# Opening of a flow-matching backbone: TensorE's order written out by hand, one filter or operand step behind each pair of modulation blocks, result tiles from two pools

## The chip, the cores and the metric

One core of a Trainium2 chip. The metric is device time in microseconds (us), lower is better; the profile is of one execution.

## The reference

One trunk layer for 128 context tokens and 256 latent tokens of width 2048, all in float32: a SwiGLU half step, a mixer (Hyena convolutions and gated DeltaNet), a second SwiGLU half step. Each sub-layer is wrapped in norms and in a modulation that comes from a conditioning vector by one large matrix. What the opening needs of it:

```
mod = silu(c) @ ada_w + ada_b                         # 2048 x 18432, for c and for c_ctx
h   = rms_norm(x, norm_pre[0]) * (1 + mod[1]) + mod[0]
x   = x + 0.5 * mod[2] * rms_norm((silu(h @ wg) * (h @ wu)) @ wd, norm_post[0])
# the Hyena filters depend on weights alone:
f    = sin(feats @ w1 + b1); f = sin(f @ w2 + b2); f = (f @ w3) * (exp(-t * |decay|) + 0.05)
spec = rfft(taps(f) / sum|taps(f)|)                   # two orders, 1024 channels, for n = 128 and 256
```

## The kernel before

A framework records the instructions in program order, then a planner orders each engine's queue by a simulated timeline, hands out tiles of the pools and sets the semaphores. `issue_after(ins)` keeps a block's instructions behind `ins` on that engine's queue; it adds no wait for a result.

The opening does three things before the first FFN can start.

- **The modulation's first two sets** (`first_mods`, L306). Shift and scale of the first sub-layer are 64 blocks of 128x1024 (512 KB) of `ada_w`, loaded on SP's queue (`first_blocks`, L292, issue L301). They lie in nine buffers, three of each of the tags that later hold the FFN's weights (raw, hi, lo). There are two passes `g` of 16 steps `kt`; each takes two blocks and multiplies them by the two conditioning vectors (L323: four matmuls, eight records in the profile, four column groups of one result tile `ada`). After a pass the result is copied by ACT (L329), transposed (L332) and turned into factors on DVE; then six `modulate` calls (L455) transpose a 128x512 piece of the tokens (L461), apply the factors on DVE (L471), and split the result into a high part on ACT and a low part on POOL (L122, L123). A pass's half of the operands `hh`, `hl` is then ready; the FFN takes the first half first.
- **The filters** (`filters`, L685). A small two-layer network of sines (L727, `sine` L667), then four turns (two orders, two halves of the channels). A turn has three steps over time pieces `t`: four matmuls into two result tiles (L759, L760), two evictions on DVE (L762), a row set to zero on POOL (L765), sum and difference on DVE (L767, L768), absolute values on ACT (L770, L771) and their sum (L772). Then come the norms (L780, eight matmuls of one column) and the spectra (L790 with ACT copies L791; L798 with ACT copies L799 and DVE L801, L802). Six stores of 256 KB a turn go to device memory (`put`, L785) from ACT's queue. The last layer's columns `w3` are loaded on POOL's queue (L707), and each turn begins by splitting its columns (L745, L746). The tiles `fh`, `wf`, `w3` have one buffer, `fev` two.
- **Tokens and small vectors** (`load_x` L256, `setup` L177). The token rows come on SP's queue behind the first four blocks. Of the small vectors the first two come on SP, the others on POOL's queue, recorded after the first yield of `setup`.

`first_mods` calls `next(work)` once behind each `kt`: three filter steps, then the vectors, then the tokens, then the filters' remaining steps. That places the work in program order only; which of them TensorE does first is the planner's choice, apart from the four matmuls of a `kt`, which are tied in pairs. Result tiles are 128x512 banks of PSUM: `aux()` (L115) takes them from a pool of three, `acc()` and `ada` from a pool of five.

The FFN's weights follow on SP's queue (L149), the first of them behind the load of block 56 and behind the filters' network (`gate`). Each unit of 512 KB is split by ACT (L122) and DVE (L123) and used in 24 matmuls (L156 to L158).

Of the kernel before, what the change touches and what calls it, by code (L numbers as in the profile page):

```python
# [11 lines left out]
F32 = mybir.dt.float32  # L12
# [7 lines left out]
P = 128  # L20
D = 2048
KT = D // P
NP_ = 128
NS = 256
T = NP_ + NS
# [8 lines left out]
HID = 64  # L34
# [70 lines left out]
class Builder:  # L105
    def __init__(self, ctx, tc, ins, outs):
        self.ctx, self.tc, self.nc = ctx, tc, tc.nc
        self.I, self.O = ins, outs
        self.side, self.rate, self.credit, self.gate, self.gd, self.hold = None, 0.0, 0.0, [], {}, None

# [3 lines left out]

    def aux(self, name="aux"):  # L115
        return self.psa.tile([P, 512], F32, tag="aux", name=name)

# [59 lines left out]
    def setup(self):  # L177
# [35 lines left out]
        o = 0  # L213
# [10 lines left out]
        for i, dst, src in loads:  # L224
            if i < 2:
                nc.sync.dma_start(out=dst, in_=src)

        def vectors(g):
            a, b = starts[g], starts[g + 1]
            pt = self.aux()  # L230
            nc.tensor.transpose(pt[:, :b - a], rt[:b - a, g, :], self.ident[:b - a, :b - a])
            nc.vector.tensor_copy(out=vec[:, a:b], in_=pt[:, :b - a])


# [7 lines left out]
        yield  # L242
        for i, dst, src in loads:
            if i >= 2:
                nc.gpsimd.dma_start(out=dst, in_=src)
        for g in range(1, len(starts) - 1):
            vectors(g)
        nc.vector.tensor_scalar(out=self.vec["gconv"], in0=self.vec["gconv"], scalar1=0.5, scalar2=None, op0=ALU.mult)
# [4 lines left out]
        nc.vector.tensor_scalar(out=self.vec["onorm"], in0=self.vec["onorm"], scalar1=0.5, scalar2=None, op0=ALU.mult)  # L253
        yield

# [49 lines left out]

    def first_mods(self, pool, blocks, hh, hl, work):  # L306


        nc = self.nc
        ab = pool.tile([P, 2, KT], F32, name="ab0")  # L310
        pre = self.vec["pre"]
        for g in range(2):

            pa = self.psm.tile([P, 512], F32, tag="mm", name="ada")
            for kt in range(KT):
                aw = [next(blocks) for m in range(2)]

                after = None
                for m in (1, 0):
                    with self.tc.issue_after(after) if after is not None else ExitStack():  # L320
                        for c in range(2):
                            q = 2 * m + c
                            mm = nc.tensor.matmul(pa[32 * q:32 * q + 32], self.cs[:, kt, :], aw[m][:, c * 512:c * 512 + 512],  # L323
                                                  start=kt == 0, stop=kt == KT - 1)
                    after = mm.ins
                next(work, None)
            gs = slice(8 * g, 8 * g + 8)
            sb = self.early(512)
            nc.scalar.copy(out=sb, in_=pa)  # L329
            pt = self.aux()  # L330
            for k in range(4):
                nc.tensor.transpose(pt[:, k * P:k * P + P], sb[:, k * P:k * P + P], self.ident)  # L332
# [9 lines left out]
            for q in (2 * g, 2 * g + 1):  # L342
                for t in range(3):
                    self.modulate(pool, self.x0[:, t, q * 512:q * 512 + 512], q, t, 0, ab, hh, hl)

# [109 lines left out]
    def modulate(self, pool, y, q, t, i, ab, hh, hl, first=False, last=False, late=None):  # L455
# [4 lines left out]
        for k in range(4):  # L460
            nc.tensor.transpose(pt[:, k * P:k * P + P], y[:, k * P:k * P + P], self.ident)  # L461
        h = pool.tile([P, 4, P], F32, tag="h", name="h", bufs=2 if i == 0 else 3)
# [222 lines left out]
    def filters(self, pool, loads):  # L685
# [37 lines left out]
        for w, src, b, dst in ((wm[:1 + 2 * BANDS, :HID], fe[:1 + 2 * BANDS], wm[:HID, HID + P:HID + P + 1], h1),  # L723
                               (wm[:HID, HID:HID + P], h1, wm[:, HID + P + 1:], h2)):
            n = dst.shape[0]
            pt = self.aux()
            nc.tensor.matmul(pt[:n, :T], w, src, start=True, stop=True)  # L727
            last = self.sine(dst, pt[:n, :T], b)
        ha = pool.tile([P, T], F32R, tag="ha", name="ha")
        hb = pool.tile([P, T], F32R, tag="hb", name="hb")  # L730
# [4 lines left out]
        nc.scalar.activation(out=dec, in_=dec, func=AF.Abs)  # L735
        yield
# [3 lines left out]
        for i, (o, half) in enumerate(turns):  # L740
            cs = slice(half * 512, half * 512 + 512)

            wf = pool.tile([P, 2, 512], F32R, tag="wf", name="wf", bufs=1)
            for d in range(2):
                nc.scalar.copy(out=wf[:, d], in_=w3[:, d])  # L745
                tt(out=wf[HID:, d], in0=w3[HID:, d], in1=wf[HID:, d], op=ALU.subtract)  # L746
            if i < 3:
                w3 = last_layer(*turns[i + 1])
# [3 lines left out]
            for t in range(3):  # L752
# [3 lines left out]
                for d in range(2):  # L756
                    pt = self.aux()
                    ts = slice(t * P, t * P + P)
                    nc.tensor.matmul(pt, ha[:, ts], wf[:, d], start=True, stop=False)  # L759
                    nc.tensor.matmul(pt, hb[:, ts], wf[:, d], start=False, stop=True)  # L760
                    h = pool.tile([P, 512], F32, tag=f"fh{d}", name="fh", bufs=1)
# [11 lines left out]
                if t == 2:  # L773
                    tt(out=ab[:, 1], in0=ab[:, 1], in1=ab[:, 2], op=ALU.add)
                yield
            pn = self.aux("pn")
            for j in range(4):
                js = slice(j * P, j * P + P)
                for t in range(2):
                    nc.tensor.matmul(pn[:, 4 * t + j:4 * t + j + 1], ab[:, t, js], self.ones[:, :1], start=True, stop=True)  # L780
            nc.vector.reciprocal(out=self.nrm[:, o, :, half * 4:half * 4 + 4], in_=pn[:, :8].rearrange("p (g c) -> p g c", g=2))

            def put(slot, ev):
                for qq in range(2):
                    nc.scalar.dma_start(out=self.spec[o, half * 2 + qq, :, slot], in_=ev[:, :, qq * 256:qq * 256 + 256])  # L785

            ev = pool.tile([P, 2, 512], F32, tag="fev", name="fev", bufs=2)
            for e in range(2):
                pt = self.aux()
                nc.tensor.matmul(pt, fwd[:, 0, e * P:e * P + P], hsd[0][:, e], start=True, stop=True)  # L790
                nc.scalar.copy(out=ev[:, e], in_=pt)  # L791
            put(2, ev)
            yield
            lo, hi = (pool.tile([P, 2, 512], F32, tag="fev", name="fev", bufs=2) for _ in range(2))
            for e in range(2):
                pp = [self.aux(), self.aux()]
                for k in range(2):
                    nc.tensor.matmul(pp[k], fwd[:, 1 + k, e * P:e * P + P], hsd[1 + k][:, e], start=True, stop=True)  # L798
# [4 lines left out]
            put(0, lo)  # L803
            put(1, hi)
            yield

# [449 lines left out]
    def run(self):  # L1256
# [7 lines left out]
        with ExitStack() as st:  # L1264
# [4 lines left out]
            with ExitStack() as s2:  # L1269
# [21 lines left out]
                load = first_loads()  # L1291
                filters = self.filters(sp, load)
                next(filters)

                def tokens():
                    next(setup)
                    yield
                    yield from load
# [3 lines left out]
                self.first_mods(sp, itertools.chain(ahead, blocks), hh, hl, work)  # L1302
                for _ in work:
                    pass
# [121 lines left out]
```

## Time and profile before

| what | us |
|---|---|
| median of 3 runs (lowest, highest) | 3276.11 (3271.34, 3278.46) |
| the profiled execution | 3268.98 |
| its span, first to last instruction | 3267.2 |
| TensorE, VectorE, ScalarE, GpSimd busy | 3184.0, 2109.1, 1070.1, 193.7 |

The span counts from the core's first instruction, and all times of rows below are us from there. PE is TensorE, DVE VectorE, ACT ScalarE, POOL GpSimd, SP SyncE; a name with q (ACTq, SPq) is the engine's own queue, in which it issues transfers. DMA queue q1 belongs to SP, q10 to ACT, q0 to POOL. PEclk is the granted clock of TensorE, where 1.00 is 2.4 GHz and 0.50 is 1.2 GHz.

### The profile page before, as it was taken

To read this page: it belongs to the slowest core of one execution; us is meant where nothing else is said; L and a number is where in the kernel's file an instruction comes from. 1 tells how busy PE (TensorE), PEld (TensorE's weight loads), DVE (VectorE), ACT (ScalarE), POOL (GpSimd) and SP (SyncE) were. 2 spreads that over 40 slices of the span, in tenths; PEclk is the share of its full clock that TensorE was granted. 3 is DMA by queue.
4 is the path that set the end of the run, shared out by engine and by line. 5 is a ranking of instruction groups with operands and counts; after the bars stand their busy time and mean duration, and the time that the engine had idled before them with its cause. 6 is when DMAs were issued, how large, how long until landed. Compare 5 with 4: busy or idle time off the path is not lost.

```text
span 3267.2 us, 43863 instructions
## 1 busy us (share of the span) xinstructions
PE 3184.0 (97%) x17409; PEld 2906.5 (89%) x17409; DVE 2109.1 (65%) x2946; ACT 1070.1 (33%) x1511; POOL 193.7 (6%) x217
## 2 busy tenths in 40 slices
PE   6899999999999999999999999989999999999998
PEld 2498999999999997999999999889899999999996
DVE  5689879797979747677657765489434434444335
ACT  4332222222222235333333333443222222222223
POOL 1200000000000001000123321020000000000001
PEclk8999999999999999999999999999999999999999
DMA  9987767676867543543422234448443344433443
GB/s 339 333 268 238 244 199 239 212 245 219 260 210 252 180 153 126 158 127 110 123 78 65 81 101 149 135 157 268 149 129 123 123 129 129 125 126 123 129 129 116
DMA packets 363206, 555.34 MB, mean 170 GB/s; under 512 B 20468, under 2 KB 265562, under 8 KB 361208
## 3 DMA queue, kind: packets, MB, share of 16 engines
q1 hardware_dynamic: 352984, 533.75, 51.0%
q0 software_dynamic: 2800, 12.32, 1.1%
q10 hardware_dynamic: 7216, 6.46, 0.6%
q8 instruction: 137, 2.24, 0.3%
q14 instruction: 69, 0.57, 0.1%
HBM read 537.21 MB, written 15.25 MB: 169 GB/s over the span
## 4 chain that ended last, share of the span: by engine, by line
PE 89%; DVE 5%; DMA 3%; issue 1%; ACT 1%; POOL 1%; SPq 0%; DVEq 0%; ACTq 0%; POOLq 0%
PE mm L158 19%; PE mm L156 19%; PE mm L157 19%; PE mt L596 8%; PE mt L594 8%; PE mt L595 8%; DMA aw<-in_ada_w_dram 2%; DVE acc L363 1%; PE pb L1140 1%; DVE lo L123 1%; PE pb L1135 1%; PE ada L323 1%; PE aux L1182 1%; PE aux L1206 1%; PE pa L370 1%
## 5 line engine op out<-in xcount | busy, mean ns | idle before, releaser
L123 DVE TENSOR_TENSOR lo<-raw,hi 128x1024 fp32r<-128x1024 f32 (+1 forms) x676 | 824.7, 1222 | 709.5 <-ACT hi L122 708.2
L122 ACT CAST hi<-raw 128x1024 fp32r<-128x1024 f32 (+1 forms) x676 | 707.5, 1047 | 1587.4 <-PE mm L157 953.0
L156 PE MATMUL mm<-hh,hi 128*128 128x384 f32 x2320 | 781.9, 338 | 5.0 <-ACT hi L122 2.7
L157 PE MATMUL mm<-hl,hi 128*128 128x384 f32 x2320 | 780.3, 336 | 0.0
L158 PE MATMUL mm<-hh,lo 128*128 128x384 f32 x2320 | 767.1, 337 | 0.6 <-DVE ss L498 0.3
L363 DVE SCALAR_TENSOR_TENSOR acc<-aw,cs,acc 128x1024 f32<-128x1024 f32 x420 | 519.9, 1277 | 27.8 <-DMA aw<-in_ada_w_dram 26.0
L157 PE MATMUL mm<-yl,hi 128*128 128x384 f32 x1408 | 470.9, 335 | 0.0
L156 PE MATMUL mm<-yh,hi 128*128 128x384 f32 x1408 | 468.3, 335 | 1.3 <-ACT yh L122 1.3
L158 PE MATMUL mm<-yh,lo 128*128 128x384 f32 x1408 | 467.3, 335 | 1.6 <-DVE lo L123 1.6
L156 PEld LDWEIGHTS mm<-hh,hi 128*128 128x128 f32 x2320 | 434.9, 188 | 11.4 <-ACT hi L122 5.7
L158 PEld LDWEIGHTS mm<-hh,lo 128*128 128x128 f32 x2320 | 432.9, 187 | 8.8 <-issue 4.6
L157 PEld LDWEIGHTS mm<-hl,hi 128*128 128x128 f32 x2320 | 434.8, 187 | 4.4 <-issue 2.5
L595 PE MATMUL mt<-hi,gl 128*128 128x512 f32 x1056 | 415.1, 393 | 0.0
L594 PE MATMUL mt<-hi,gh 128*128 128x512 f32 x1056 | 414.9, 393 | 0.0
L596 PE MATMUL mt<-lo,gh 128*128 128x512 f32 x1056 | 398.9, 393 | 1.2 <-DVE lo L123 1.1
L156 PEld LDWEIGHTS mm<-yh,hi 128*128 128x128 f32 x1408 | 264.4, 188 | 2.1 <-ACT yh L122 1.7
L158 PEld LDWEIGHTS mm<-yh,lo 128*128 128x128 f32 x1408 | 264.4, 188 | 1.9 <-DVE lo L123 1.9
L157 PEld LDWEIGHTS mm<-yl,hi 128*128 128x128 f32 x1408 | 264.8, 188 | 0.6 <-POOL yl L123 0.2
L596 PEld LDWEIGHTS mt<-lo,gh 128*128 128x128 f32 x1056 | 198.3, 188 | 48.8 <-DVE lo L123 2.5
L594 PEld LDWEIGHTS mt<-hi,gh 128*128 128x128 f32 x1056 | 198.3, 188 | 48.1 <-issue 2.5
L595 PEld LDWEIGHTS mt<-hi,gl 128*128 128x128 f32 x1056 | 198.3, 188 | 43.8
L627 DVE TENSOR_TENSOR yacc<-mt,yacc 128x512 f32<-128x512 f32 x192 | 128.3, 684 | 134.9 <-PE mt L596 134.9
(349 smaller groups left out, 2421.5 us busy)
## 6 DMA issues: line engine op xcount, KB each, us to landing
aw<-in_ada_w_dram SPq DMA_DIRECT2D x288, 512.0 KB, 4.5
raw<-in_ffn_wg_dram SPq DMA_DIRECT2D x176, 512.0 KB, 4.4
raw<-in_ffn_wu_dram SPq DMA_DIRECT2D x176, 512.0 KB, 3.6
raw<-in_ffn_wd_dram SPq DMA_DIRECT2D x176, 512.0 KB, 3.6
raw<-in_w_in_dram SPq DMA_DIRECT2D x112, 512.0 KB, 3.6
raw<-in_w_out_dram SPq DMA_DIRECT2D x32, 512.0 KB, 3.7
spec<-fev ACTq DMA_DIRECT2D x24, 256.0 KB, 7.1
grow<-gate POOLq DMA_DIRECT2D x3, 2048.0 KB, 7.8
```

What stands on the lines that cost most here:

```text
L122: self.nc.scalar.copy(out=hi, in_=src)
L123: return (eng or self.nc.vector).tensor_tensor(out=lo, in0=src, in1=hi, op=ALU.subtract)
L156: t.matmul(out, hi[:, k, c], xh, start=first, stop=False)
L157: t.matmul(out, hi[:, k, c], xl, start=False, stop=False)
L158: t.matmul(out, lo[:, k, c], xh, start=False, stop=last)
L323: mm = nc.tensor.matmul(pa[32 * q:32 * q + 32], self.cs[:, kt, :], aw[m][:, c * 512:c * 512 + 512], start=kt == 0, stop=kt == KT - 1)
L363: nc.vector.scalar_tensor_tensor(out=d, in0=aw, scalar=self.cs[:, kt, v:v + 1], in1=d, op0=ALU.mult, op1=ALU.add)
L370: nc.tensor.matmul(pa[32 * q:32 * q + 32, :], self.pick[:, v], acc[:, v, q * 512:q * 512 + 512], start=v == 0, stop=v == 1)
L594: mm(pts[t], xh[:, ts], hi[:, k], start=first, stop=False)
L595: mm(pts[t], xl[:, ts], hi[:, k], start=False, stop=False)
L596: mm = mm(pts[t], xh[:, ts], lo[:, k], start=False, stop=last)
L627: nc.vector.tensor_tensor(out=y, in0=pt, in1=y, op=ALU.add)
```

## The change

- **Order by hand.** `self.newest` holds TensorE's last recorded instruction of the opening. The matmuls of a `kt` and the step behind it are each recorded under `issue_after(self.newest)`, so TensorE's queue is: group of a `kt`, its step, the next group, its step, and so on. The order ends with the second pass.
- **Finer steps by a plan.** `filters` yields after each matmul of the network, after each `t`, after the first spectra, after the norms, and after each half of the other spectra: 30 steps, of seven per turn. What follows a pass (`spectra`) is a generator too: the factors, then the six modulations in pairs. `plan` lists what stands behind each of the 32 `kt`: one filter step behind most, and in the second pass's first eight the operand steps of the first pass alternate with filter steps. The second pass's own operand steps come after the order has ended.
- **Result tiles.** While the order holds, `aux()` takes tiles from the pool of three and the pool of five in turn.
- **Queues.** The 24 stores of the spectra go from ACT's queue to POOL's. The first `w3` (two transfers) goes from POOL's queue to SP's. The small vectors' loads are recorded at the start.
- **Columns.** The next turn's columns are split in the third `t` step of a turn instead of at the turn's start. The norms stand behind the first spectra.

```diff
     def aux(self, name="aux"):
+        if self.turns is not None and next(self.turns):
+            return self.psm.tile([P, 512], F32, tag="mm", name=name)
         return self.psa.tile([P, 512], F32, tag="aux", name=name)
...
         for i, dst, src in loads:
-            if i < 2:
-                nc.sync.dma_start(out=dst, in_=src)
+            (nc.sync if i < 2 else nc.gpsimd).dma_start(out=dst, in_=src)
...
-    def first_mods(self, pool, blocks, hh, hl, work):
+    def first_mods(self, pool, blocks, hh, hl, plan):
...
+        def behind():
+            return self.tc.issue_after(self.newest) if self.newest is not None else ExitStack()
+
+        def spectra(pa, g):
...
+            yield mm.ins
+            for n, (q, t) in enumerate((q, t) for q in (2 * g, 2 * g + 1) for t in range(3)):
+                self.modulate(pool, self.x0[:, t, q * 512:q * 512 + 512], q, t, 0, ab, hh, hl)
+                if n % 2:
+                    yield self.turned.ins
...
+                for m in (1, 0):
+                    with behind():
+                        for c in range(2):
+                            q = 2 * m + c
+                            mm = nc.tensor.matmul(pa[32 * q:32 * q + 32], self.cs[:, kt, :], aw[m][:, c * 512:c * 512 + 512],
+                                                  start=kt == 0, stop=kt == KT - 1)
+                    self.newest = mm.ins
+                for step in next(plan):
+                    with behind():
+                        self.newest = next(half if step is None else step, None) or self.newest
+            half = spectra(pa, g)
+        self.newest, self.turns = None, None
+        for _ in half:
+            pass
...
-                nc.gpsimd.dma_start(out=w3[r * HID:r * HID + HID],
+                (nc.sync if o == half == 0 else nc.gpsimd).dma_start(out=w3[r * HID:r * HID + HID],
...
                 if t == 2:
                     tt(out=ab[:, 1], in0=ab[:, 1], in1=ab[:, 2], op=ALU.add)
-                yield
+                    if i < 3:
+                        wf = columns(w3)
+                yield mm.ins
...
             def put(slot, ev):
                 for qq in range(2):
-                    nc.scalar.dma_start(out=self.spec[o, half * 2 + qq, :, slot], in_=ev[:, :, qq * 256:qq * 256 + 256])
+                    nc.gpsimd.dma_start(out=self.spec[o, half * 2 + qq, :, slot], in_=ev[:, :, qq * 256:qq * 256 + 256])
...
-                work = itertools.chain(itertools.islice(filters, 3), tokens(), filters)
+                self.turns = itertools.cycle((0, 1))
+                f = self.filters(sp, load)
+                next(f)
+                h = None
+                plan = iter([[], [f, f, f, f, load], [setup, load], [f], [f], [f], [f], [f], [f], [f], [f], [f], [f], [f], [f], [f],
+                             [h], [f], [h], [f], [h], [f], [h], [f], [f], [f], [f], [f], [f], [f], [f], [f]])
```

## Rows read from the trace of the kernel before

**Rows 1.** The page: span, and busy time of the engines

```profile
span 3267.2 us, 43863 instructions
...
PE 3184.0 (97%) x17409; PEld 2906.5 (89%) x17409; DVE 2109.1 (65%) x2946; ACT 1070.1 (33%) x1511; POOL 193.7 (6%) x217
```

**Rows 2.** Windows of 20 us: busy us of each engine, PEclk, DMA share, GB/s

```profile
140.00:160.00 20.00, 18.98 (x118) 14.71 (x117) 12.20 (x32) 6.60 (x9) 6.54 (x4) 1.00 0.85 302
...
180.00:200.00 20.00, 20.00 (x117) 20.00 (x116) 16.39 (x19) 6.95 (x9) 0.00 (x0) 1.00 0.81 256
```

**Rows 3.** Timeline of TensorE, 130 to 147 us: start, duration, what

```profile
137.85 2.82 PE L798 MATMUL aux<-slot,early 128*128 128x512 f32 x6
...
140.61 1.06 PE L323 MATMUL ada<-aw,cs 128*32 128x512 f32 x8
...
142.66 1.92 PE L323 MATMUL ada<-aw,cs 128*32 128x512 f32 x16
...
146.26 0.44 PE L156 MATMUL mm<-hh,hi 128*128 128x384 f32 x1 [0.29 <-ACT hi L122]
```

**Rows 4.** Line 301 from 134 to 135 us: the last block's issue and landing

```profile
L301 SPq DMA_DIRECT2D aw<-in_ada_w_dram x1: 327/327/327, 134.3 to 134.3; - x1
...
DMA to landing us min/median/max: 5.3/5.3/5.3
```

**Rows 5.** Windows of unequal length, columns as in rows 2

```profile
60.00:92.00 32.00, 24.12 (x102) 8.80 (x98) 15.55 (x26) 9.96 (x16) 2.79 (x5) 0.82 1.02 363
...
92.00:96.00 4.00, 3.23 (x19) 0.79 (x12) 2.38 (x5) 2.87 (x6) 0.00 (x0) 0.76 0.53 165
...
136.00:140.00 4.00, 4.00 (x23) 2.62 (x20) 0.30 (x2) 0.58 (x1) 0.00 (x0) 1.00 0.96 357
...
140.00:144.00 4.00, 4.00 (x28) 0.87 (x26) 0.00 (x0) 0.58 (x1) 0.00 (x0) 1.00 0.42 147
```

**Rows 6.** Waits of SP's queue, 0 to 170 us: us, times, longest

```profile
SPq L301 <- PE ada L323: 56.4, 22, 5.8
```

**Rows 7.** The chain that ended last, 38 to 84 us: start, duration, what

```profile
38.42 1.93 PE ada L323 x8
...
66.02 12.54 DMA spec<-fev
...
80.26 2.08 PE aux L798 x2
```

**Rows 8.** Timeline of ACT, 64 to 82 us

```profile
70.89 1.07 ACT L791 COPY fev<-aux 128x512 f32<-128x512 f32 x2 [1.33 <-DMA spec<-fev]
...
78.64 0.89 ACTq L785 DMA_DIRECT2D spec<-fev  x2
```

**Rows 9.** DMA queues, 40 to 60 us: packets, MB, share of 16 engines

```profile
q1 hardware_dynamic: 1806, 6.58, 84.7%
...
q0 software_dynamic: 160, 0.52, 9.9%
```

**Rows 10.** DMA queues, 104 to 140 us

```profile
q1 hardware_dynamic: 2940, 10.21, 78.0%
...
q10 hardware_dynamic: 2859, 2.75, 21.9%
```

**Rows 11.** Line 707, POOL's loads of the columns: issue ns, min/median/max

```profile
L707 POOL DMA_DIRECT2D w<-in_hy_f_w_dram x8: 587/604/798, 1.4 to 68.5; - x8
```

**Rows 12.** Timeline, 56 to 84 us: DVE's first addition of two steps

```profile
56.11 0.69 DVE L767 TENSOR_TENSOR slot<-fh 128x512 f32<-128x512 f32 x1 [0.69 <-POOL fh L765]
...
60.70 0.69 DVE L767 TENSOR_TENSOR slot<-fh 128x512 f32<-128x512 f32 x1 [0.67 <-POOL fh L765]
```

**Rows 13.** Groups of DVE, 28 to 140 us: busy us, mean ns, idle before

```profile
L802 DVE TENSOR_TENSOR fev<-fev,aux 128x512 f32<-128x512 f32 x6 | 4.1, 678 | 0.0
```

**Rows 14.** Timeline of POOL, 144 to 162 us

```profile
151.73 3.03 POOL L123 TENSOR_TENSOR hl<-h,hh 128x512 fp32r<-128x512 f32 x1 [23.07 <-ACT hh L122]
...
159.06 1.29 POOL L123 TENSOR_TENSOR hl<-h,hh 128x512 fp32r<-128x512 f32 x1 [0.86 <-ACT hh L122]
```

More of the change, by code (lines that the diff above doesn't have):

```diff
@@ L108, in __init__ @@
         self.I, self.O = ins, outs
-        self.side, self.rate, self.credit, self.gate, self.gd, self.hold = None, 0.0, 0.0, [], {}, None
+        self.side, self.rate, self.credit, self.gate, self.gd, self.hold, self.turns = None, 0.0, 0.0, [], {}, None, None
     def pool(self, stack, name, bufs=1, **kw):
@@ L230, in vectors @@
             pt = self.aux()
-            nc.tensor.transpose(pt[:, :b - a], rt[:b - a, g, :], self.ident[:b - a, :b - a])
+            mm = nc.tensor.transpose(pt[:, :b - a], rt[:b - a, g, :], self.ident[:b - a, :b - a])
             nc.vector.tensor_copy(out=vec[:, a:b], in_=pt[:, :b - a])
+            return mm
         vectors(0)
@@ L242, in setup @@
         yield
-        for i, dst, src in loads:
-            if i >= 2:
-                nc.gpsimd.dma_start(out=dst, in_=src)
         for g in range(1, len(starts) - 1):
-            vectors(g)
+            mm = vectors(g)
         nc.vector.tensor_scalar(out=self.vec["gconv"], in0=self.vec["gconv"], scalar1=0.5, scalar2=None, op0=ALU.mult)
@@ L311, in first_mods @@
         pre = self.vec["pre"]
[L312 to L326, printed above, removed]
+        self.newest = None
+        def behind():
+            return self.tc.issue_after(self.newest) if self.newest is not None else ExitStack()
+        def spectra(pa, g):
             gs = slice(8 * g, 8 * g + 8)
@@ L331, in first_mods @@
             for k in range(4):
-                nc.tensor.transpose(pt[:, k * P:k * P + P], sb[:, k * P:k * P + P], self.ident)
+                mm = nc.tensor.transpose(pt[:, k * P:k * P + P], sb[:, k * P:k * P + P], self.ident)
             src = pt.rearrange("p (k m c v) -> p m c k v", k=4, m=2, c=2)
@@ L341, in first_mods @@
                                                op0=ALU.add, op1=ALU.mult)
-            for q in (2 * g, 2 * g + 1):
-                for t in range(3):
-                    self.modulate(pool, self.x0[:, t, q * 512:q * 512 + 512], q, t, 0, ab, hh, hl)
+            yield mm.ins
[3 more added lines that the diff above has]
+                    yield self.turned.ins
+        for g in range(2):
+            pa = self.psm.tile([P, 512], F32, tag="mm", name="ada")
+            for kt in range(KT):
+                aw = [next(blocks) for m in range(2)]
+                for m in (1, 0):
[12 more added lines that the diff above has]
+            pass
     def ada(self, m, pool, after=None):
@@ L460, in modulate @@
         for k in range(4):
-            nc.tensor.transpose(pt[:, k * P:k * P + P], y[:, k * P:k * P + P], self.ident)
+            self.turned = nc.tensor.transpose(pt[:, k * P:k * P + P], y[:, k * P:k * P + P], self.ident)
         h = pool.tile([P, 4, P], F32, tag="h", name="h", bufs=2 if i == 0 else 3)
@@ L726, in filters @@
             pt = self.aux()
-            nc.tensor.matmul(pt[:n, :T], w, src, start=True, stop=True)
+            mm = nc.tensor.matmul(pt[:n, :T], w, src, start=True, stop=True)
             last = self.sine(dst, pt[:n, :T], b)
+            yield mm.ins
         ha = pool.tile([P, T], F32R, tag="ha", name="ha")
@@ L739, in filters, with columns @@
         tt = nc.vector.tensor_tensor
-        for i, (o, half) in enumerate(turns):
-            cs = slice(half * 512, half * 512 + 512)
+        def columns(w3):
             wf = pool.tile([P, 2, 512], F32R, tag="wf", name="wf", bufs=1)
@@ L746, in filters @@
                 tt(out=wf[HID:, d], in0=w3[HID:, d], in1=wf[HID:, d], op=ALU.subtract)
+            return wf
+        wf = columns(w3)
+        for i, (o, half) in enumerate(turns):
+            cs = slice(half * 512, half * 512 + 512)
             if i < 3:
@@ L759, in filters @@
                     nc.tensor.matmul(pt, ha[:, ts], wf[:, d], start=True, stop=False)
-                    nc.tensor.matmul(pt, hb[:, ts], wf[:, d], start=False, stop=True)
+                    mm = nc.tensor.matmul(pt, hb[:, ts], wf[:, d], start=False, stop=True)
                     h = pool.tile([P, 512], F32, tag=f"fh{d}", name="fh", bufs=1)
@@ L774, in filters, with put @@
                     tt(out=ab[:, 1], in0=ab[:, 1], in1=ab[:, 2], op=ALU.add)
-                yield
+                    if i < 3:
+                        wf = columns(w3)
+                yield mm.ins
+            def put(slot, ev):
+                for qq in range(2):
+                    nc.gpsimd.dma_start(out=self.spec[o, half * 2 + qq, :, slot], in_=ev[:, :, qq * 256:qq * 256 + 256])
+            ev = pool.tile([P, 2, 512], F32, tag="fev", name="fev", bufs=2)
+            for e in range(2):
+                pt = self.aux()
+                mm = nc.tensor.matmul(pt, fwd[:, 0, e * P:e * P + P], hsd[0][:, e], start=True, stop=True)
+                nc.scalar.copy(out=ev[:, e], in_=pt)
+            put(2, ev)
+            yield mm.ins
             pn = self.aux("pn")
@@ L779, in filters @@
                 for t in range(2):
-                    nc.tensor.matmul(pn[:, 4 * t + j:4 * t + j + 1], ab[:, t, js], self.ones[:, :1], start=True, stop=True)
+                    mm = nc.tensor.matmul(pn[:, 4 * t + j:4 * t + j + 1], ab[:, t, js], self.ones[:, :1], start=True, stop=True)
             nc.vector.reciprocal(out=self.nrm[:, o, :, half * 4:half * 4 + 4], in_=pn[:, :8].rearrange("p (g c) -> p g c", g=2))
-            def put(slot, ev):
-                for qq in range(2):
-                    nc.scalar.dma_start(out=self.spec[o, half * 2 + qq, :, slot], in_=ev[:, :, qq * 256:qq * 256 + 256])
[L787 to L793, printed above, removed]
+            yield mm.ins
             lo, hi = (pool.tile([P, 2, 512], F32, tag="fev", name="fev", bufs=2) for _ in range(2))
@@ L797, in filters @@
                 for k in range(2):
-                    nc.tensor.matmul(pp[k], fwd[:, 1 + k, e * P:e * P + P], hsd[1 + k][:, e], start=True, stop=True)
+                    mm = nc.tensor.matmul(pp[k], fwd[:, 1 + k, e * P:e * P + P], hsd[1 + k][:, e], start=True, stop=True)
                 nc.scalar.copy(out=lo[:, e], in_=pp[0])
@@ L802, in filters @@
                 tt(out=lo[:, e], in0=lo[:, e], in1=pp[1], op=ALU.add)
-            put(0, lo)
-            put(1, hi)
-            yield
+                if e:
+                    put(0, lo)
+                    put(1, hi)
+                yield mm.ins
     def conv3(self, u, pt, w):
@@ L1291, in run @@
                 load = first_loads()
[L1292 to L1298, printed above, removed]
-                work = itertools.chain(itertools.islice(filters, 3), tokens(), filters)
+                self.turns = itertools.cycle((0, 1))
[4 more added lines that the diff above has]
+                             [h], [f], [h], [f], [h], [f], [h], [f], [f], [f], [f], [f], [f], [f], [f], [f]])
                 hh, hl = self.operands()
-                self.first_mods(sp, itertools.chain(ahead, blocks), hh, hl, work)
-                for _ in work:
+                self.first_mods(sp, itertools.chain(ahead, blocks), hh, hl, plan)
+                for _ in f:
                     pass
```

1 line of the change is left out of this document (removed).

## The prediction

> **What bounds the kernel now.** The page first: over the whole span TensorE is busy 97% [rows 1], so what happens elsewhere counts only where it lets TensorE start its long run earlier. The windows come next. From 180 us on TensorE is busy 20.00 of 20 us, from 140 to 160 it is busy 18.98 [rows 2]; the first FFN matmul stands at 146.26 us [rows 3]. So the change is worth what it moves that start, and little else: behind it the same matmuls follow without a gap.
>
> What sets 146.26? The opening's TensorE groups, each eight records behind two blocks of 512 KB. The last block is issued at 134.3 us and lands 5.3 us later, at 139.6 [rows 4]. The last groups are not done then: the order that the planner chose puts six spectra matmuls at 137.85, one group at 140.61, two more spectra matmuls, and the last two groups only at 142.66, ending at 144.58 [rows 3]. TensorE is thus 5.0 us behind the data. Before that the DMA engines are the limit: busy 1.02 in 60:92 and 0.96 in 136:140, with two holes, 0.53 in 92:96 and 0.42 in 140:144 [rows 5]. The second hole lies behind the last block; the SP queue's waits say why both exist: it waits for the group of a block whose buffer it wants, 56.4 us in 22 times [rows 6]. Most of that is free, as nine buffers are then full of work for the DMA engines; a hole opens when TensorE is late by more than the ring holds.
>
> The first hole can be followed back. A spec store issued on ACT's queue at 66.02 took 12.54 us to land, and the spectra matmuls that stood next on TensorE came at 80.26 [rows 7]. Between them ACT copied at 70.89 and then sat before its next two stores until 78.64 [rows 8]: the wait is one of ACT's queue, and TensorE's fixed order passed it on to the groups.
>
> **The change part by part.** *Order.* Each group of a block pair is now followed by exactly one step, and the next group stands behind that step. Nothing is computed more or less, so the sum has only the waits.
>
> First term, the hole at 92:96: 4 us at 0.53 is 1.9 us; 136:140 gives 0.2 [rows 5]. Both should close if no step holds TensorE longer than the ring: 2.1 us.
>
> Second term, slow transfer while busy. In 40:60 queue q1 moved 6.58 MB with 84.7% of 20 us, 2.57 us per MB; in 104:140 10.21 MB with 78.0% of 36 us, 2.75 us per MB [rows 9, 10]. The first is a stretch where blocks queue deeply, the second one where SP waited for buffers. With the ring kept full, the 19 or so MB from block 28 on could cost 0.18 us per MB less, 3.4 us; if the cause is another, nothing. I take the middle, 1.7, since the two stretches also differ in the number of stores.
>
> Third term, TensorE's lag at the end. One group takes 1.06 us [rows 3]. In the new order only one filter step stands between the last two groups. I put the end of the last group 1.6 us behind its data in place of 5.0: 3.4 us. Bounds: 0 if the steps run late as now, 3.9 if only the group itself is left.
>
> *Stores on POOL's queue.* 24 stores leave ACT's queue for POOL's, which frees ACT from the 7-us stop above. On POOL an issue of this size cost 0.60 us in the opening [rows 11]: 24 by 0.6 is 14.4 us of POOL over some 100 us, beside its eight memsets and the operands' subtractions. A store that waits for its data now holds POOL; behind it stand the memset of a later filter step and that step's DVE additions. Program order puts every store ahead of that memset, and the data is there first. I cost it at nothing; its cover is that a turn of the filters has time to spare. From rows: DVE's first addition of a step comes at 56.11 and again at 60.70 [rows 12], so a step takes 4.6 us, three 13.8; four evictions of 0.68 [rows 13], one addition of 0.69 and a pair of ACT copies of 1.1 [rows 8] make 18.3 us a turn. A turn has seven steps, and a pair of blocks comes every 3.37 us (29 pairs from the group at 38.42 [rows 7] to about 136): 23.6 us. So 5.3 us a turn are free.
>
> For the transfer itself the nearest rows on either side are the store on ACT's queue, 21.9% of 36 us for 2.75 MB, 2.87 us per MB [rows 10], and POOL's loads of 64 partitions, 9.9% of 20 us for 0.52 MB, 3.8 [rows 9]. At the second price 6.3 MB would cost 5.9 us more. I take no difference, since shape and packets of the stores stay as they are in the first row; below the first a gain isn't excluded, but none is counted. The Trainium skill (DMA: Bandwidth & Descriptors, Issuing engines are not separate DMA queues) says that transfers of all issuing engines share the same engines, and that another issuer saves issue time alone; the two rates of this trace for different issuers, 2.87 and 3.8, differ with the shape and don't contradict it.
>
> *Loads.* Two issues of the first filter columns go from POOL to SP, ahead of the decay row and of the first four blocks; eleven small loads on POOL move up by these two issues, 1.2 us. The bytes are the same and the DMA engines are saturated until the token rows are in, so: nothing, with 0.7 us either way for two issues of 0.33 on SP [rows 4].
>
> *Six result tiles.* With three tiles TensorE can be three results ahead of DVE; with six it can pass a step whose readers are late. This is what makes the fixed order bearable, as a step writes two. DVE's own work in a turn is under the 23.6 us above, so it isn't the limit. The FFN's four accumulators come from the same pool; at worst the first waits for the last two evictions, 1.4 us, hidden by the first cast of weights.
>
> *Finer steps, columns one step earlier, modulation in pairs.* The same instructions at other places, so nothing but order; the first half's six modulations now lie on every second pair of blocks.
>
> Sum: 2.1 + 1.7 + 3.4 = 7.2 us. The profiled execution would go from 3268.98 to 3261.8; it lies 7.1 below the median of the runs shown, which I take as the base: 3276.11 - 7.2 = **3268.9 us**. The planner also re-orders what follows; I allow 2 us either way. A measurement here can tell about 0.2%, 6.6 us.
>
> **The rivals.** *Hidden by the DMA engines.* The holes close but the transfers stay as slow, or the late steps take their place elsewhere; then only part of the lag at the end goes: 1 to 5 us, 3273 in the middle. For it: busy shares of 0.96 to 1.02 over nearly all of the stretch [rows 5]. Against: the hole at 140:144 and the lag of 5.0 us stand outside that bound.
>
> *The ring really full.* All of the second term, the best end of the third and shorter steps: 2.1 + 3.4 + 3.9 = 9.4, with 2 us of luck in the later order 11 and more: 3264.5. For it: the rate of 2.57 us per MB was reached. Against: it was reached before the stores began in earnest.
>
> *POOL becomes the step's clock.* One subtraction on POOL took 3.03 us while DVE was busy, the same one 1.29 later [rows 14]. If the stores' issues were lengthened by the same 1.74 us, six per turn would cost 10.4 us on POOL, the memset behind them would come late, and the turn would lose 10.4 - 5.3 = 5.1 us: 20.4 us over four turns. Nine blocks of 0.524 MB at 2.57 us per MB cover 12.1 of it; 8.3 us reach the last block, the holes and the lag stay: 3284.4, **slower**. It decides where an issue costs over 0.8 us more than 0.6. Against it: POOL's loads were issued in 0.59 to 0.80 us in the same stretch, among the same DVE work [rows 11]. The Trainium skill (SBUF — State Buffer, the passage on "DVE blocks DMA") speaks for this rival: descriptors of a POOL-issued DMA are written through a port that some DVE modes lock. The subtraction's 3.03 us agrees with such a lock, the 0.80 us of the slowest issue does not show it; the sum stays with the issues' own row.
>
> *The order doesn't bind.* If the planner already kept nearly this order, nothing changes. But it stood six matmuls ahead of a ready group [rows 3, 4], so the change does what it says; I count this in the first rival.
>
> **How the numbers follow.** Forecast (a gain of 5 to 9.5) 0.55, of which 0.37 lies over 6.6 us; hidden by the DMA engines 0.20; ring really full 0.13; POOL the clock 0.12. Faster 0.37 + 0.13 = 0.50; no change 0.18 + 0.20 = 0.38; slower 0.12. The range leaves out most of the slower rival and the upper part of the third: 3262 to 3279. Its upper end also takes in half of the 5.9 us for the stores' dearer transfer, and 2 us of later order.
>
> **What would show it.** Right: groups with the last block at 142 us or less; the first FFN matmul at 138 to 141 us; no stretch of 4 us under 0.9 of the DMA engines between 60 us and the last block; POOL's issues near 0.6 us; no wait of ACT for a store. Wrong: TensorE waiting on DVE or ACT ahead of a group for several us (a step too slow for its place), a spec store whose landing holds DVE's evictions, issues on POOL over 1.4 us, or an opening that is shorter while the later stages lose as much.

## The result and the profile after

The change made the kernel slower: 3298.30 us (median of 4 runs, 3295.94 to 3300.41) against 3274.82 beside them (3271.34 to 3278.46), a ratio of 1.0071 [1.0059, 1.0083]. The forecast was 3268.9, with a range to 3279. The profiled execution took 3295.94.

The page of the kernel after, span and busy times, then two of its DMA queues (packets, MB, share of 16 engines over the span); compare [rows 1]:

```profile
span 3294.2 us, 43859 instructions
...
PE 3186.1 (97%) x17409; PEld 2911.9 (88%) x17409; DVE 2112.7 (64%) x2946; ACT 1069.8 (32%) x1511; POOL 208.7 (6%) x239
...
q0 software_dynamic: 4560, 18.09, 1.6%
...
q10 hardware_dynamic: 688, 0.17, 0.0%
```

TensorE's work is the same and the span is 27.0 us longer. TensorE's timeline of the kernel after, in two stretches of the opening (start, duration, line, tiles, count, and in brackets the idle time ahead with its releaser):

```profile
66.24 0.50 PE L779 MATMUL aux<-wf,ha 128*128 128x512 f32 x1
...
74.52 1.07 PE L350 MATMUL ada<-aw,cs 128*32 128x512 f32 x8
75.52 0.38 PE L814 MATMUL pn<-base,fab 128*128 128x1 f32 x2
84.77 3.15 PE L814 MATMUL pn<-base,fab 128*128 128x1 f32 x14 [8.87 <-DVE fab L794]
87.84 1.93 PE L350 MATMUL ada<-aw,cs 128*32 128x512 f32 x8
...
148.89 0.38 PE L814 MATMUL pn<-base,fab 128*128 128x1 f32 x2
157.93 3.15 PE L814 MATMUL pn<-base,fab 128*128 128x1 f32 x14 [8.65 <-DVE fab L794]
161.00 1.93 PE L350 MATMUL ada<-aw,cs 128*32 128x512 f32 x8
...
167.84 0.74 PE L158 MATMUL mm<-hh,hi 128*128 128x384 f32 x1
```

The last line answers to 146.26 in [rows 3]: the first FFN matmul is 21.6 us later, most of the whole loss. From it to the end took 3120.9 us before and 3126.4 after. In the thirteen profiled executions of this case that remainder lies between 3120.4 and 3128.5, so a few us of any single profile can't be laid to the opening.

The place is the norms, `pn` (L814): eight matmuls, sixteen records. The first reads an operand that is already there; the other seven stand for 6 to 10 us until DVE's last sum (L794), with all groups behind them. The waits of the kernel after, 0 to 170 us (us, times, longest):

```profile
PE pn L814 <- DVE fab L794: 33.9, 4, 9.9
...
DVE slot L787 <- POOL fh L785: 9.5, 5, 3.7
```

Four turns, four waits. In the kernel before, the planner had put four records of the spectra and two groups between the first matmul of the norms and the others, and none of them waits:

```profile
66.86 0.59 PE L780 MATMUL pn<-base,fab 128*128 128x1 f32 x2
67.31 3.31 PE L790 MATMUL aux<-slot,early 128*128 128x512 f32 x4
70.55 1.92 PE L323 MATMUL ada<-aw,cs 128*32 128x512 f32 x16
72.41 1.72 PE L780 MATMUL pn<-base,fab 128*128 128x1 f32 x14
```

In the changed kernel's last turn, the group at 161.00 stands behind the norms although its blocks had landed at 149.8. The last block is later too; its issue and landing, against 134.3 and 5.3 in [rows 4]:

```profile
L300 SPq DMA_DIRECT2D aw<-in_ada_w_dram x1: 327/327/327, 144.0 to 144.0; - x1
...
DMA to landing us min/median/max: 8.4/8.4/8.4
```

It lands at 152.4, 12.8 us later than before. So 12.8 of the 21.6 us were lost while blocks still came, and the rest behind them. Windows of 20 us show how the first part was lost (columns as in [rows 2]). The kernel before:

```profile
80.00:100.00 20.00, 13.85 (x58) 4.17 (x58) 12.18 (x22) 8.05 (x14) 1.04 (x2) 0.83 0.90 314
...
120.00:140.00 20.00, 17.13 (x83) 7.02 (x76) 12.55 (x21) 6.15 (x10) 1.03 (x2) 0.83 1.00 366
```

The kernel after, and four us behind its second wait:

```profile
80.00:100.00 20.00, 15.23 (x62) 6.94 (x62) 8.10 (x13) 4.44 (x8) 2.92 (x5) 0.69 0.80 271
...
120.00:140.00 20.00, 14.64 (x64) 7.04 (x65) 9.82 (x20) 4.56 (x8) 4.36 (x4) 0.66 0.62 219
...
88.00:92.00 4.00, 4.00 (x11) 1.22 (x8) 0.16 (x1) 0.18 (x1) 0.00 (x0) 0.50 0.34 91
```

The DMA engines' share falls from 0.90 and 1.00 to 0.80 and 0.62. The nine buffers feed them through most of a wait; the hole comes just behind it, 0.34 in 88:92. Over the five windows from 40 to 140 us the engines are busy for 87.0 us in place of 99.2, about as much less as the last block is late. PEclk is lower too: 0.50 from 84 to 88 us, at the end of the wait. At 1.2 GHz the fourteen records take 3.15 us, where sixteen take 1.95 in e3 below, and the group behind them 1.93 instead of 1.07: some 2 us more than at the full clock. Not all of that is the wait's, as a kernel without it also has groups at the lower clock (1.94 us in e3).

What DVE does meanwhile, the timeline of the same turn:

```profile
69.86 0.69 DVE L787 TENSOR_TENSOR slot<-fh 128x512 f32<-128x512 f32 x1 [1.56 <-POOL fh L785]
...
72.37 1.29 DVE L761 TENSOR_TENSOR wf<-w,wf 64x512 fp32r<-64x512 f32 x2 [1.22 <-ACT wf L760]
...
77.73 0.69 DVE L787 TENSOR_TENSOR slot<-fh 128x512 f32<-128x512 f32 x1 [2.02 <-POOL fh L785]
...
81.25 0.69 DVE L787 TENSOR_TENSOR slot<-fh 128x512 f32<-128x512 f32 x1
...
84.02 0.69 DVE L794 TENSOR_TENSOR fab<-fab 128x512 f32<-128x512 f32 x1
```

The three time steps begin with TensorE's matmul at 66.24 and end with this sum at 84.71: 18.5 us. TensorE was at the norms after 9.3 us. In the chain DVE also makes the next turn's columns (L761), 1.29 us behind a wait of 1.22 for ACT; no run took them out. And DVE is twice late for POOL; POOL's timeline says why:

```profile
66.41 2.90 POOL L801 DMA_DIRECT2D spec<-fev  x4 [16.75 <-DVE fev L824]
69.31 0.52 POOL L785 MEMSET fh<- 1x512 f32 x1
...
75.72 1.46 POOL L801 DMA_DIRECT2D spec<-fev  x2 [0.56 <-ACT fev L807]
77.18 0.51 POOL L785 MEMSET fh<- 1x512 f32 x1
```

Stores that waited for their data are issued at 0.73 us each, and the memset that DVE waits for stands behind them.

### The profile page after: what moved, and what is told of

Its sections match the earlier page's. It is cut to its first block, busy times and chain, and to the rows that moved or that the text cites. A ratio compares the mean times of both kernels' runs of the same rounds, so it can differ in the third digit from the quotient of the medians.

```text
span 3294.2 us, 43859 instructions
## 1 busy us (share of the span) xinstructions
PE 3186.1 (97%) x17409; PEld 2911.9 (88%) x17409; DVE 2112.7 (64%) x2946; ACT 1069.8 (32%) x1511; POOL 208.7 (6%) x239
## 3 DMA queue, kind: packets, MB, share of 16 engines
q0 software_dynamic: 4560, 18.09, 1.6%
## 4 chain that ended last, share of the span: by engine, by line
PE 87%; DVE 6%; DMA 3%; issue 2%; ACT 1%; POOL 1%; SPq 0%; DVEq 0%; ACTq 0%; POOLq 0%
PE mm L160 18%; PE mm L158 18%; PE mm L159 18%; PE mt L611 8%; PE mt L609 8%; PE mt L610 8%; DMA aw<-in_ada_w_dram 2%; DVE acc L378 2%; DVE lo L125 1%; PE pb L1164 1%; PE pb L1159 1%; PE aux L1206 1%; PE aux L1230 1%; PE aux L821 1%; DMA early<-in_posc_dram 1%
```

## The experiments

The theory: the norms stand one step behind the third time step, too close for the DVE chain that feeds them; in a fixed order that wait holds the groups, the ring and the DMA engines. Rivals: the chain of the three steps is itself the turn's bound, the stores on POOL are the loss, or the result tiles are. Times are medians of 4 to 10 runs, ratios are to the kernel before.

### The wait itself

**e5: norms that read constants.** The matmuls at L814 keep their place and count:

```diff
-  mm = nc.tensor.matmul(pn[...], ab[:, t, js], self.ones[:, :1], start=True, stop=True)
+  mm = nc.tensor.matmul(pn[...], self.ones, self.ones[:, :1], start=True, stop=True)
```

> The changed kernel, with the norms' matmuls reading the constant ones in place of the sums of absolute values, so the normalisation of the filters is left out; their place in TensorE's order, their number and shape stay. If TensorE's wait for that one operand is the loss: the waits at the norms vanish, the next wait is at the first half of the spectra and as short as in the run with the norms last (under 12 us in total), and the time is 3262 to 3272 us. If the order is dear for another reason (the place of the step in itself, the finer steps, the stores): above 3285 us.

Measured: 3263.81 us, 0.9971 [0.9960, 0.9981], first FFN matmul at 140.6. TensorE's largest wait of this kernel:

```profile
PE ada L350 <- DMA aw<-in_ada_w_dram: 30.5, 16, 8.2
```

The wait at `pn` is gone and the groups wait for their blocks instead. One operand turned a gain of 0.3% into a loss of 0.7%.

**e3: norms behind the spectra.** The same arithmetic, two steps later (three steps then lie between the third time step and the norms, not the four that the expectation counts):

```diff
-            pn = self.aux("pn")
-            ... eight matmuls, reciprocal, yield mm.ins
             lo, hi = ...
             ... the second spectra, in two steps
+            pn = self.aux("pn")
+            ... eight matmuls, reciprocal, yield mm.ins
```

> The changed kernel with the norms moved two steps later, behind the second half of the spectra, so that four steps and not one lie between the third time step and the norms. If the place of the norms alone is at fault: the 33.9 us of waits shrink to under 10, 3275 to 3283 us. Chain theory: the spectra (their first half) need the third time step's sum and difference, which are ready only some 2 us before the norms' operand, so TensorE waits there instead; 3288 to 3298 us, with the waits now at the spectra's matmuls.

Measured: 3264.1 us, 0.9970 [0.9958, 0.9982], first FFN matmul at 137.87. The time is below both ranges that I had expected. TensorE's timeline in its second turn:

```profile
72.39 1.12 PE L814 MATMUL aux<-slot,early 128*128 128x512 f32 x2
74.86 1.12 PE L814 MATMUL aux<-slot,early 128*128 128x512 f32 x2 [1.34 <-DVE slot L787]
...
80.76 1.95 PE L827 MATMUL pn<-base,fab 128*128 128x1 f32 x16
83.50 1.94 PE L350 MATMUL ada<-aw,cs 128*32 128x512 f32 x8 [0.80 <-DMA aw<-in_ada_w_dram]
```

The spectra now wait 1.34 us for an operand that DVE makes earlier in the chain, and the norms run through in 1.95 us. The windows that had the holes:

```profile
80.00:100.00 20.00, 18.68 (x100) 7.46 (x92) 10.93 (x24) 5.59 (x9) 3.92 (x6) 0.83 1.01 392
120.00:140.00 20.00, 16.45 (x89) 7.31 (x88) 13.28 (x25) 8.07 (x13) 3.36 (x5) 1.00 0.89 333
```

The last block lands at 132.4, in the second window. The rival that the chain bounds the turn (3288 to 3298) falls: this turn went from 61.08 to 85.37, 24.3 us, and the DMA engines were full throughout, at 1.01 and more in each 4 us.

**e4: another plan.** From the second turn on, the three time steps stand together, then three groups with nothing between, then the rest one by one:

```diff
-  ... [f], [f], [f], [f], [f], [f], [f], ...
+  ... [f, f, f, f], [], [], [], [f], [f], [f], ...
```

> The changed kernel with another plan and nothing else: the three time steps of a turn stand together behind one group, then three groups follow with no filter step (in the second pass: with operand steps), then the rest of the turn one by one. The order is still fixed by hand and the work the same. Chain theory: the chain has three groups' time to finish, TensorE's waits at the norms fall below 10 us in total, and the time is 3268 to 3282 us. If a fixed order is dear by itself, or POOL's stores are: 3290 us and more.

Measured: 3287.84 us, 1.0041 [1.0026, 1.0056], first FFN matmul at 163.2; the norms still wait 26.4 us in 4 times, of which 7.0 in the first turn, whose plan is as in the change. I had expected 3268 to 3282. The profile shows the error:

```profile
68.29 3.64 PE L350 MATMUL ada<-aw,cs 128*32 128x512 f32 x32
```

Four groups whose blocks had landed pass in 3.64 us. I had counted a group as a pair's 3.4 us of DMA time. A group that is ready buys DVE only 0.9 us.

**e2: the change without the fixed order.** The steps are not tied to the groups; the ties inside a pair stay as before.

```diff
-                    with behind():
+                    with self.tc.issue_after(after) if after is not None else ExitStack():
...
-                    with behind():
-                        self.newest = next(half if step is None else step, None) or self.newest
+                    next(half if step is None else step, None)
```

> The changed kernel without the order written by hand: steps and groups are recorded in the same program order, but only the four matmuls of one group stay tied in pairs as before; tiles, finer steps, queues and columns stay as changed. Chain theory: the planner again lets other work and groups pass the norms, the wait of TensorE at the norms falls below 10 us, and the time is 3268 to 3278 us. POOL theory, or a cost in the other parts: it stays above 3290 us.

Measured: 3268.61 us, 0.9985 [0.9975, 0.9994], first FFN matmul at 144.8. The largest of the norms' waits for that operand in this kernel:

```profile
PEld pn L814 <- DVE fab L794: 3.8, 4, 1.9
```

With everything else of the change kept, the norms' weight loads wait 3.8 us in 4 times instead of 34.2; what is left is a small gain.

**e6: three result tiles.** The fixed order as in the change, with results from the pool of three:

```diff
-                self.turns = itertools.cycle((0, 1))
```

> The changed kernel with results from the pool of three alone; the order by hand stays. Theory that the six tiles make the wait (they let TensorE run ahead of DVE into the norms): TensorE waits at the time steps for a free tile instead, the norms' waits fall below 20 us, but the sum of both and the time stay the same within 4 us, 3294 to 3302. Rival (my forecast's view, that six tiles make the fixed order bearable): with three the groups stand behind waits for tiles too, and the time is 3305 us or more.

Measured: 3281.58 us, 1.0032 [1.0020, 1.0043], first FFN matmul at 154.0: fewer tiles made the changed kernel faster, by 13.8 us at that matmul. I had expected no difference within 4 us, with 3305 and more as the rival: both missed. Its waits of TensorE:

```profile
PE pn L814 <- DVE fab L794: 13.0, 4, 4.3
...
PE aux L779 <- DVE fh L782: 7.2, 4, 4.6
```

With three tiles TensorE is held in short pieces at the time steps, so that it comes later to the norms, where it stands 13.0 us instead of 33.9. The two waits together are 20.2 us, so the wait was not only moved. That TensorE with six tiles runs ahead through ready groups, and stops with the ring behind it, is how I read the two traces; no run shows it apart.

### The stores

**e1: the change with the stores on ACT's queue.**

```diff
-                    nc.gpsimd.dma_start(out=self.spec[...], ...)
+                    nc.scalar.dma_start(out=self.spec[...], ...)
```

> The changed kernel with one edit undone: the 24 stores of the spectra are issued on ACT's queue again. Chain theory (TensorE's fixed order brings it to the norms 4 to 10 us before DVE, ACT and POOL have finished the three time steps that the norms need; 33.9 us of such waits in the profile after): only the memsets that stand behind stores on POOL come earlier, DVE's wait for them falls from 9.5 us to about 5, and the time is 3293 to 3298 us. POOL theory (the stores on POOL delay the memsets, and this makes the chain too slow): the waits at the norms fall by more than half and the time is 3275 to 3283 us.

Measured: 3290.04 us, 1.0046 [1.0028, 1.0064], first FFN matmul at 164.8, norms' wait 30.0 us. DVE's additions wait 3.3 us for the memset instead of 9.5. By the ratios the queue cost 0.0025, some 8 us; by the first FFN matmul of the two profiles 3.1 us. The intervals just overlap, so its share lies somewhere between nothing and these 8 us, and most of the loss remains without it. The time lies between the two ranges expected; the waits at the norms, which the POOL theory wanted more than halved, went from 33.9 to 30.0.

**e11: the kernel before with its stores on POOL's queue**, the same edit the other way round.

> The kernel before with one edit: the 24 stores of the spectra are issued from POOL's queue, as in the change; nothing else of the change is in it. The prediction held that this costs nothing, as a turn of the filters has time to spare, and that it frees ACT from its stop of 7 us: 3268 to 3276 us. Theory, from the two pairs of kernels that differ only in the stores' queue (8 us and 3 us dearer on POOL): the memset of a step stands behind the stores on POOL and DVE's additions behind the memset, so 3276 to 3283 us. Rival: in the planner's own order TensorE is not tied to the late step, so the loss is hidden and the time stays within 2 us of before.

Measured: 3272.59 us, 0.9993 [0.9979, 1.0007]: no difference; the rival held. In this kernel (rows of its waits, and its stores' issue in ns, min/median/max)

```profile
DVE slot L767 <- POOL fh L765: 4.6, 7, 0.7
```

```profile
L785 POOL DMA_DIRECT2D spec<-fev x24: 725/725/1494, 47.4 to 154.3; - x24
```

the issues are as long, but DVE never waits more than 0.7 us for a memset. So if the stores cost the changed kernel a few us (e1), it should be by standing ahead of a step on which a fixed order hangs. This run also bears on the forecast's first hole: with ACT free of the stores the DMA share in 92:96 is 1.00 in place of 0.53, another stretch is at 0.81 (128:132), and the time is the same within an interval wider than that term's 1.9 us. Closing that one hole gained nothing that shows.

**e7: norms behind the spectra, and stores on ACT's queue** (the edits of e3 and e1).

> The kernel with the norms two steps later, and the stores back on ACT's queue. If the memsets behind POOL's stores cost time also where TensorE does not wait at the norms: 3258 to 3262 us, 3 to 6 below the run with the norms last. If ACT's stop at its stores comes back (up to 7 us in the kernel before): 3266 to 3272. If the DMA engines are the limit there and neither matters: 3262 to 3266.

Measured: 3261.07 us, 0.9962 [0.9947, 0.9977], faster than both kernels. Against e3 (0.9970) the intervals overlap. Its spectra wait 10.3 us for DVE in 4 pieces, none longer than 3.7, and no time is lost by it that shows.

### Order and tiles once nothing waits

**e8: e3 without the fixed order** (the edits of e3 and e2).

> The kernel with the norms two steps later and without the order by hand. If the planner's order is as good as one by hand once no step waits: 3262 to 3268 us, as with the order. If the order by hand is worth something by itself (TensorE's lag at the last blocks, 3.4 us in the forecast): 3266 to 3272, above the run with the order.

Measured: 3269.27 us, 0.9983 [0.9973, 0.9992]. The median is 5.2 us above e3's, but the intervals (to 0.9982 and from 0.9973) just overlap, so this pair doesn't show that the fixed order is worth something. In its favour, all five kernels with the fixed order and without the norms' wait (e3, e5, e7, e9, e10) have ratios of 0.9962 to 0.9973, and the two without the order 0.9983 (e8) and 0.9985 (e2).

**e9: e3 with three result tiles** (the edits of e3 and e6).

> The norms stay two steps later, as in the kernel that lost its waits, and the opening's results come from the pool of three alone. Theory: the six tiles did harm only because TensorE ran ahead into a step that waits; without that wait the number of tiles decides little, since TensorE is held by the blocks anyway: 3261 to 3268 us, within 3 us of the same order with six tiles (3264.1). Rival A, what the prediction said: six tiles make the fixed order bearable, so with three TensorE waits for DVE's evictions and the opening gets longer: 3270 us or more, with several us of waits of the steps' matmuls on DVE. Rival B: fewer tiles are better in any order, 3258 us or less.

Measured: 3264.6 us, 0.9973 [0.9961, 0.9985], first FFN matmul at 136.9. The number of tiles makes no difference here that shows; TensorE's waits on DVE's evictions at L779 were 5.5 us in 4 times.

**e10: e7 with three result tiles** (the edits of e3, e1 and e6).

> Norms two steps later, stores on ACT's queue as before the change, three result tiles. Theory: as the same order with six tiles (3261.1), within 3 us. Rival A: the evictions on ACT stand behind stores on its queue, and with three tiles TensorE cannot pass them, as in the kernel before (a stop of ACT of 7 us): 3268 us or more, with TensorE waiting on ACT's evictions of the spectra.

Measured: 3265.53 us, 0.9970 [0.9959, 0.9981]. It isn't told apart from e7: the medians differ by 4.5 us, more than the 3 I had allowed, but the intervals overlap. Rival A's 3268 was not reached. Its profiled execution was 9 us above its median, so I read little from it.

## Why the prediction was wrong

**The step that failed** is the cover of the filters' turn: "18.3 us a turn" of chain against "23.6 us" of pace, "So 5.3 us a turn are free." It was set against the wrong time. The chain of the three time steps feeds a step on TensorE's own queue, the norms, and what TensorE has until then is not seven steps but four. By the prediction's own pace these are 4 x 3.37 = 13.5 us, less than the chain, even if only its three steps of 4.6 us and the last addition are counted, 14.5: a wait would have shown without a new measurement. And TensorE doesn't keep that mean pace. In the turn above it did four steps and four groups in 9.3 us, because blocks had piled up; e4 shows four ready groups in 3.64 us. So 18.5 us of chain stood against 9.3 us of TensorE, and the norms waited 8.87. The wait seems to feed itself, as blocks pile up during it: from the end of the first wait at 57.2 us to 102 us no group waits for its blocks. No run shows that part alone. The prediction listed this sign ("a step too slow for its place") and gave it no price and no chance; its slower rival was another mechanism.

That 18.3 came so near to the 18.5 measured is luck. 2.7 of the 18.3 are DVE's four results of the spectra, which lie outside the stretch measured; in it stand instead the waits for the memsets and for the columns, so that DVE's first additions are 7.87 and 3.52 us apart, not 4.6.

**Six result tiles**, "what makes the fixed order bearable", did the opposite: e6 is faster with three, and e9 shows no use for six where nothing waits. The Trainium skill (Perfetto Trace Analysis, Optimization Strategy) reads the same gap repeated on an engine that should be saturated as possibly too little SBUF or PSUM for the next tile. Here such a gap came four times, at the norms, and fewer tiles made it shorter (33.9 to 13.0 us in all): the measurement decides against that reading in this case.

**POOL's stores.** The issue was forecast at 0.60 us and took 0.73, at most 1.20 in the changed kernel; the rival's 1.4 us was not reached, so POOL did not become the step's clock. That they cost nothing held in the planner's order (e11). In the fixed one it is open (e1 against the change, up to some 8 us), and there "the data is there first" was wrong: the stores waited for TensorE's late spectra and then stood four in a row, 2.90 us, ahead of the memset.

**The three terms of the gain** show in the kernels whose wait is gone. The holes close: e3's DMA share is 1.01 in 80:100. The last group's end, put 1.6 us behind its data, is 3.8 behind it in e3 (136.14 against 132.36), so the third term gave 1.2 of its 3.4 us. For the transfers' price, four kernels, DMA queues from 90 to 120 us (packets, MB, share). The kernel before:

```profile
q1 hardware_dynamic: 2215, 8.04, 76.9%
```

e3, fixed order, stores on POOL (q0):

```profile
q1 hardware_dynamic: 2851, 10.39, 88.2%
q0 software_dynamic: 480, 1.57, 13.0%
```

e7, fixed order, stores on ACT (q10):

```profile
q1 hardware_dynamic: 2798, 10.20, 87.0%
q10 hardware_dynamic: 1632, 1.57, 14.9%
```

e11, the planner's order, stores on POOL:

```profile
q1 hardware_dynamic: 2431, 8.84, 81.4%
q0 software_dynamic: 480, 1.57, 15.2%
```

Share x 30 us / MB gives the blocks 2.87, 2.55, 2.56 and 2.76 us per MB. The stores' queue doesn't decide the price (e3 and e7). The order alone doesn't either: in the same stretch e2, without the fixed order, has 2.55, and e10, with it, 2.83. Why a block costs more in some kernels isn't settled. Where it fell, the second term's middle, 1.7 us, was too low: e3 and e7 lie 0.19 below the 2.75 of [rows 10], and over 19 MB that is 3.6 us, about the upper bound the term had kept; against the 2.87 of the same stretch it would be more.

By e3's profile the terms were thus wrong one by one and near in the sum: the last block lands 7.2 us sooner, where the first two terms gave 3.8, and the lag behind it gave 1.2 in place of 3.4. In all, e3, e5, e7, e9 and e10 gained 0.27 to 0.38% where 0.22% was forecast. So the gain was there to be had, and the change gave it back, three times over, in a wait of its own.

## What to carry to other kernels

Before a fixed order ties a step to its place, compare for each step the time from its producer's first instruction to its operand with the time in which the engine gets from one to the other at its fastest, not at the mean pace of the loop; where it doesn't fit, move the reader back, as the norms here by two steps. More result buffers are no cure for such a wait: here they made it longer, and where nothing waited they made no difference that showed. Taking the dependence out of one instruction, at the same place and count, shows in one run what a wait is worth.

## What the runs showed of the hardware

- The same 24 stores of 256 KB, 6.29 MB, go in packets of different size by queue. The POOL and ACT queues of e7, whose stores are on ACT (packets, MB, share over the span), against 4560 and 688 packets on the page above:

```profile
q0 software_dynamic: 2640, 11.80, 1.1%
q10 hardware_dynamic: 7216, 6.46, 0.6%
```

  On POOL's queue the stores take 1920 packets, 3.3 KB each; on ACT's 6528, 0.96 KB each. From 90 to 120 us they cost the DMA engines 2.85 us per MB on ACT's queue (e7) and 2.48 to 2.90 on POOL's (e3, e11). The prediction had taken packets and price as unchanged. The Trainium skill (DMA: Bandwidth & Descriptors, Issuing engines are not separate DMA queues) counts only issue time as the difference between issuers; here the packets differ as well.
- In the wait of 8.87 us TensorE's granted clock went to 0.50, at 1.2 GHz; the group behind the norms and the spectra behind it still ran at that level, and a group at 93.00 took 1.06 us again. A long wait is not all that can stand ahead of such a fall: e3 has 0.50 in the same 4 us, and the longest idle time of its TensorE in the 12 us before them is 1.34 us. Both kernels, 84 to 88 us, the changed one first (columns as in [rows 2]):

```profile
84.00:88.00 4.00, 3.23 (x18) 3.22 (x22) 0.74 (x2) 0.00 (x0) 0.00 (x0) 0.50 1.01 409
```

```profile
84.00:88.00 4.00, 4.00 (x16) 1.37 (x12) 1.21 (x2) 0.63 (x1) 0.00 (x0) 0.50 1.03 412
```
